# A branch over sixty no-ops at the head of VectorE's program, and a dead copy taken out, in a rotary-embedding kernel

## The chip, the core and the metric

The kernel runs on one core of a Trainium2 chip. The metric is the device time of one execution in microseconds (us); lower is better. A time is a median over several runs, and one further execution is recorded by the hardware profiler: its profile and its trace are what the text reads.

## The reference

`x` has the shape (16, 512, 1024) in float32: 16 sequences of 512 positions, each position a row of 16 heads of 64 numbers. Every head is split into its first and its second half of 32 numbers and rotated by tables of cos and sin that depend on the position alone:

```python
x = x.reshape(batch, seq, num_heads, head_dim)
x1, x2 = x[..., :half_dim], x[..., half_dim:]
cos = cos[None, :, None, :]
sin = sin[None, :, None, :]
rotated = np.concatenate([x1 * cos - x2 * sin, x1 * sin + x2 * cos], axis=-1)
```

The arithmetic is small. 33.6 MB are read and 33.6 MB are written.

## The kernel before

**Tiles.** The rows are cut into eight tiles of 4 MB. A tile holds two sequences: 128 partitions, and in each partition eight positions ("rows" `r` = 0 to 7) of 1024 numbers. A tile `x_sb` is loaded, changed in place and stored. Five buffers (`NB`) hold tiles.

**The tables.** `sin` and `cos` are loaded by ScalarE's queue into 64 partitions (`tabs`, L73 and L74). The tables have to stand in all 128 partitions, and TensorE does that: GpSimd makes an identity matrix `ident` (L80, L81), VectorE builds from it a selecting matrix `sel` and its negative (L86 to L88), and three products (L93 to L95) give `sns_ps` (−sin, +sin) and `cos_ps` (cos) in PSUM. ScalarE copies `sns_ps` to `sns` in SBUF (L99), since GpSimd works from there, and `cos_ps` to `cost` (L100). Nothing reads `cost`.

**The work on a tile** (`compute`). For every position, x times cos is added to x with its halves swapped times (−sin, +sin).
- Rows 0 and 1 (`PEROWS`): GpSimd makes the second product `B` of row 0, VectorE that of row 1 (L126). VectorE makes the first product in place (L136). TensorE adds the two by products with `ident` (L141, L142), and ScalarE copies the sums back (L143).
- Rows 2 to 7 in three pairs (`PAIRS`): GpSimd makes the second product `T` (L131), VectorE the first one into PSUM (`pp`, L147) and the sum (L148).

**Order.** The schedule is the program's order (`manual_schedule`). All transfers of x stand on SyncE's queue in one order: load 0 in four pieces, loads 1 to 4, stores 0 to 2, loads 5 to 7, stores 3 to 6, and the last store in four pieces. A load into a buffer that is used again waits for that buffer's store. At the start each engine takes part in a barrier and runs over one branch to its own part of the program (L191 in the trace); at the end SyncE waits for the last stores (also L191).

```python
    for t in range(NB):
        compute(t)
        if t < NT - NB:
            store(t)
    for t in range(NB, NT):
        load(t)
```

Of the kernel before, what the change touches and what calls it, by code (L numbers as in the profile page):

```python
# [7 lines left out]
FP32 = mybir.dt.float32  # L8
# [4 lines left out]
def kernel(  # L13
# [8 lines left out]
    nc = tc.nc  # L22
    P = nc.NUM_PARTITIONS
# [3 lines left out]
    half = hd // 2  # L27
# [4 lines left out]
    R = seq // HP  # L32
# [2 lines left out]
    NB = 5  # L35
    PAIRS = (2, 4, 6)
    PEROWS = (0, 1)

    xv = x.rearrange("b (p r) d -> (b p) (r d)", r=R)
    xv = xv.rearrange("(t p) f -> t p f", p=P)  # L40
# [5 lines left out]
    fixed = ctx.enter_context(tc.tile_pool(name="fixed", bufs=1))  # L46
# [28 lines left out]
    for t in range(1, NB):  # L75
        load(t)


    ident = fixed.tile([P, P], FP32, name="ident")
    nc.gpsimd.memset(ident, 0.0)  # L80
    nc.gpsimd.affine_select(  # L81
        out=ident, in_=ident, compare_op=ALU.not_equal, fill=1.0,
        base=0, pattern=[[-1, P]], channel_multiplier=1,
    )
    sel = fixed.tile([HP, 2, P], FP32, name="sel")
    nc.vector.tensor_copy(out=sel[:, 0, :HP], in_=ident[:HP, :HP])  # L86
    nc.vector.tensor_copy(out=sel[:, 0, HP:], in_=ident[:HP, :HP])
# [3 lines left out]
    cos_ps = ptab.tile([P, R, half], FP32, name="cos_ps")  # L91
# [3 lines left out]
    nc.tensor.matmul(out=cos_ps.rearrange("p r j -> p (r j)"), lhsT=sel[:, 0, :], rhs=tabs[:, 0],  # L95
                     start=True, stop=True)
    sns = fixed.tile([P, R, 2, half], FP32, name="sns")
    cost = fixed.tile([P, R, half], FP32, name="cost")
    nc.scalar.copy(out=sns, in_=sns_ps)  # L99
    nc.scalar.copy(out=cost, in_=cos_ps)  # L100

    def view(ap, r0, n):

        return ap[:, r0 * dim:(r0 + n) * dim]
# [5 lines left out]
    def snsb(tab, r0, n):  # L110
        return bass.AP(tensor=tab.tensor, offset=tab.offset + r0 * hd,
                       ap=[tab.ap[0], [hd, n], [0, nh], [1, hd]])

    def swapped(xt, r0, n):
        return bass.AP(tensor=xt.tensor, offset=xt.offset + r0 * dim + half,
                       ap=[xt.ap[0], [hd, n * nh], [-half, 2], [1, half]])

    def compute(t):
# [3 lines left out]

        for r in PEROWS:
            B = bpool.tile([P, dim], FP32, name="B")
            eng = nc.vector if r == PEROWS[-1] else nc.gpsimd
            eng.tensor_tensor(out=B, in0=swapped(xt, r, 1), in1=snsb(sns_ps if eng is nc.vector else sns, r, 1),  # L126
# [6 lines left out]

        for r in reversed(PEROWS):
            xr = view(xt, r, 1)
# [60 lines left out]
```

## Time and profile before

| | |
|---|---|
| median of 3 runs | 162.91 us (162.82 to 163.51) |
| profiled execution, its own time | 162.99 us |
| its span in the trace | 161.0 us |
| VectorE (DVE) busy | 137.8 us, 86% |
| GpSimd (POOL) busy | 127.1 us, 79% |
| TensorE (PE) busy | 78.3 us, 49% |
| ScalarE (ACT) busy | 21.0 us, 13% |
| HBM read and written | 33.69 MB and 33.55 MB, 418 GB/s over the span |
| SyncE's DMA queue, share of 16 DMA engines | 97.6% |

In the profile "L126" is line 126 of the kernel and "x_sb<-T,pp" an instruction that writes x_sb from T and pp. A line of a group or of the timeline names start or busy time, engine, line and operation, and in square brackets how long the engine had been idle before and who released it. A digit of the slices is the busy share of 1/40 of the span in tenths. In the DMA queues, a line is the queue's number and kind, then packets, MB and the share of the 16 DMA engines' time. "SPq" is SyncE's queue, "q14 instruction" the loading of program code. Where the text speaks of the trace's records, it means the single instructions, transfer packets and landings that the trace holds beneath these views, with their times in ns.

### The profile page before, as it was taken

What the parts mean: (1) busy time and instruction counts of PE and PEld (TensorE: products, weight loads), DVE (VectorE), ACT (ScalarE), POOL (GpSimd) and SP (SyncE); (2) the same over time, 40 slices, a digit from 0 to 9 for tenths busy, and PEclk for the clock granted to TensorE, in tenths of its full rate; (3) what the DMA queues carried; (4) which work ended last, traced back from release to release, by engine and by line L of the source; (5) the groups of instructions that cost most, each with busy time, mean ns of one, the idle gap of its engine ahead of it and who ended that gap; (6) DMA issues with size and microseconds to landing.
All of it is one profiled execution on the core that took longest, in us unless ns stands there. A gap on an engine that the chain in (4) does not pass through costs nothing. (4 is left out here: it accounts for less than half of the span.)

```text
span 161.0 us, 581 instructions
## 1 busy us (share of the span) xinstructions
PE 78.3 (49%) x134; PEld 32.3 (20%) x134; DVE 137.8 (86%) x75; ACT 21.0 (13%) x35; POOL 127.1 (79%) x38
## 2 busy tenths in 40 slices
PE   0449900598019910894049700990079803991000
PEld 0223300233014400341024200340034202340000
DVE  1077999999999999999999999999999999999400
ACT  3021210014001210022002300121001400121000
POOL 1079999999998799959995999869995999692000
PEclk9999996569755985589957995699655975598555
DMA  5999999999999999999999999999999999999994
GB/s 181 385 419 480 391 497 415 391 472 440 391 456 456 391 432 480 391 415 489 399 417 472 407 415 464 415 407 472 423 399 456 448 399 456 448 391 417 421 423 187
DMA packets 3329, 67.25 MB, mean 418 GB/s; under 512 B 384, under 2 KB 512, under 8 KB 512
## 3 DMA queue, kind: packets, MB, share of 16 engines
q1 hardware_dynamic: 3168, 67.11, 97.6%
q10 hardware_dynamic: 160, 0.13, 0.3%
q14 instruction: 1, 0.01, 0.0%
HBM read 33.69 MB, written 33.55 MB: 418 GB/s over the span
## 5 line engine op out<-in xcount | busy, mean ns | idle before, releaser
L131 POOL TENSOR_TENSOR T<-x_sb,sns 128x2048 f32<-128x2048 f32 x24 | 108.2, 4526 | 10.5 <-DVE x_sb L148 10.5
L141 PE MATMUL ps<-x_sb,ident 128*128 128x512 f32 x64 | 44.8, 790 | 61.0 <-issue 40.4
L148 DVE TENSOR_TENSOR x_sb<-T,pp 128x2048 f32<-128x2048 f32 x24 | 54.9, 2288 | 3.4 <-POOL T L131 1.0
L147 DVE TENSOR_TENSOR pp<-x_sb,cos_ps 128x2048 f32<-128x2048 f32 x24 | 55.0, 2294 | 0.6
L142 PE MATMUL ps<-B,ident 128*128 128x512 f32 x64 | 40.3, 717 | 0.0
L143 ACT COPY x_sb<-ps 128x512 f32<-128x512 f32 x32 | 18.8, 586 | 117.6 <-PE ps L142 117.6
L141 PEld LDWEIGHTS ps<-x_sb,ident 128*128 128x128 f32 x64 | 15.2, 253 | 83.3 <-issue 80.4
L126 POOL TENSOR_TENSOR B<-x_sb,sns 128x1024 f32<-128x1024 f32 x8 | 18.8, 2346 | 7.6 <-ACT sns L99 7.6
L142 PEld LDWEIGHTS ps<-B,ident 128*128 128x128 f32 x64 | 15.4, 241 | 22.0 <-issue 22.0
L136 DVE TENSOR_TENSOR x_sb<-x_sb,cos_ps 128x1024 f32<-128x1024 f32 x16 | 18.8, 1218 | 0.5
L126 DVE TENSOR_TENSOR B<-x_sb,sns_ps 128x1024 f32<-128x1024 f32 x8 | 9.7, 1217 | 7.0 <-ACT sns L99 7.0
L93 PE MATMUL sns_ps<-tabs,sel 64*128 64x256 f32 x2 | 1.2, 697 | 6.2 <-DMA tabs<-in_sin_dram 6.2
L93 PEld LDWEIGHTS sns_ps<-tabs,sel 64*128 64x128 f32 x2 | 0.5, 310 | 6.1 <-issue 6.1
L99 ACT ACT_TABLE_LOAD x1 | 1.3, 1283 | 1.9 <-issue 1.9
L86 DVE COPY sel<-ident 64x64 f32<-64x64 f32 x1 | 0.2, 185 | 1.3 <-POOL ident L81 1.3
L99 ACT COPY sns<-sns_ps 128x512 f32<-128x512 f32 x1 | 0.6, 586 | 5.0 <-PE sns_ps L94 5.0
L95 PE MATMUL cos_ps<-tabs,sel 64*128 64x256 f32 x2 | 1.2, 711 | 0.0
L94 PE MATMUL sns_ps<-tabs,sel 64*128 64x256 f32 x2 | 1.1, 631 | 0.0
L94 PEld LDWEIGHTS sns_ps<-tabs,sel 64*128 64x128 f32 x2 | 0.7, 334 | 0.2
L95 PEld LDWEIGHTS cos_ps<-tabs,sel 64*128 64x128 f32 x2 | 0.5, 306 | 0.6 <-DMA tabs<-in_cos_dram 0.6
L100 ACT COPY cost<-cos_ps 128x256 f32<-128x256 f32 x1 | 0.4, 373 | 0.5 <-PE cos_ps L95 0.5
L80 POOL MEMSET ident<- 128x128 f32 x1 | 0.2, 204 | 0.3 <-POOLq L177 0.3
(7 smaller groups left out, 1.1 us busy)
## 6 DMA issues: line engine op xcount, KB each, us to landing
x_sb<-in_x_dram SPq DMA_DIRECT2D x7, 4096.0 KB, 29.5
out_dram<-x_sb SPq DMA_DIRECT2D x7, 4096.0 KB, 27.0
x_sb<-in_x_dram SPq DMA_DIRECT2D x4, 1024.0 KB, 8.7
out_dram<-x_sb SPq DMA_DIRECT2D x4, 1024.0 KB, 9.2
tabs<-in_sin_dram ACTq DMA_DIRECT2D x1, 64.0 KB, 5.3
tabs<-in_cos_dram ACTq DMA_DIRECT2D x1, 64.0 KB, 6.7
```

The costliest lines, as they stand in the source:

```text
L93: nc.tensor.matmul(out=sns_ps[:, :, 1, :], lhsT=sel[:, 0, :], rhs=sin3, start=True, stop=True)
L94: nc.tensor.matmul(out=sns_ps[:, :, 0, :], lhsT=sel[:, 1, :], rhs=sin3, start=True, stop=True)
L95: nc.tensor.matmul(out=cos_ps.rearrange("p r j -> p (r j)"), lhsT=sel[:, 0, :], rhs=tabs[:, 0], start=True, stop=True)
L99: nc.scalar.copy(out=sns, in_=sns_ps)
L126: eng.tensor_tensor(out=B, in0=swapped(xt, r, 1), in1=snsb(sns_ps if eng is nc.vector else sns, r, 1), op=ALU.mult)
L131: nc.gpsimd.tensor_tensor(out=T, in0=swapped(xt, r0, 2), in1=snsb(sns, r0, 2), op=ALU.mult)
L136: nc.vector.tensor_tensor(out=xr, in0=xr, in1=cosb(cos_ps, r, 1), op=ALU.mult)
L141: nc.tensor.matmul(out=ps, lhsT=ident, rhs=xc, start=True, stop=False)
L142: nc.tensor.matmul(out=ps, lhsT=ident, rhs=bc, start=False, stop=True)
L143: nc.scalar.copy(out=xc, in_=ps)
L147: nc.vector.tensor_tensor(out=pp, in0=xr, in1=cosb(cos_ps, r0, 2), op=ALU.mult)
L148: nc.vector.tensor_tensor(out=xr, in0=ts[r0], in1=pp, op=ALU.add)
```

## The change

Behind the two instructions that make `ident`, VectorE gets a register set to 0 and a conditional block that is entered if the register is above 0, which it never is. In the block stand 60 no-ops. The block divides the program: each engine's instructions are now in a part before it and a part behind it. In the built program that places a plain branch on every engine: on SyncE behind the first of the four pieces of load 0, on ScalarE between the loads of sin and cos, on GpSimd between the two instructions on `ident`, on TensorE at the head. VectorE has, at its head, two register moves, the compare-and-branch, the 60 no-ops and the block's closing branch. The rest of the program keeps its order on every engine.

The copy of `cos_ps` to `cost` is gone, and the tile with it. VectorE's first product with cos (L136), which waited for ScalarE because of that copy, waits for TensorE instead.

```diff
+    PAD = 60
...
-
     ident = fixed.tile([P, P], FP32, name="ident")
     nc.gpsimd.memset(ident, 0.0)
     nc.gpsimd.affine_select(
         out=ident, in_=ident, compare_op=ALU.not_equal, fill=1.0,
         base=0, pattern=[[-1, P]], channel_multiplier=1,
     )
+
+
+    step = nc.vector.alloc_register("step")
+    nc.vector.reg_mov(step, 0)
+    with tc.If(nc.vector.snap(step) > 0):
+        for _ in range(PAD):
+            nc.vector.nop(hint="pad")
+
+
     sel = fixed.tile([HP, 2, P], FP32, name="sel")
...
     sns = fixed.tile([P, R, 2, half], FP32, name="sns")
-    cost = fixed.tile([P, R, half], FP32, name="cost")
     nc.scalar.copy(out=sns, in_=sns_ps)
-    nc.scalar.copy(out=cost, in_=cos_ps)
```

## The prediction

> **What bounds the kernel now.** I read the page first: busy shares, the slices, the DMA queues.
>
> ```profile
> PE 78.3 (49%) x134; PEld 32.3 (20%) x134; DVE 137.8 (86%) x75; ACT 21.0 (13%) x35; POOL 127.1 (79%) x38
> ...
> DMA  5999999999999999999999999999999999999994
> ...
> q1 hardware_dynamic: 3168, 67.11, 97.6%
> ...
> q14 instruction: 1, 0.01, 0.0%
> ```
>
> No compute engine is full, the 16 DMA engines are: 97.6% of the span goes to SyncE's queue, and only the first and last slice are not full. One packet of the span is not data but program code (q14). Next, the waits of SyncE's queue and the end of the chain of waits:
>
> ```profile
> SPq L64 <- DMA out_dram<-x_sb: 17.7, 2, 9.5
> ...
> SPq L191 <- DMA out_dram<-x_sb: 9.0, 4, 2.4
> ```
>
> ```profile
> 148.31 2.29 DVE x_sb L148
> ```
>
> The last compute instruction ends at 150.60 of 160.97, so the chain holds only compute and leaves 10.4 us to the transfers. At the end SyncE waits for the four pieces of the last store; by the trace's records they are through at 152.83, 155.26, 157.71 and 160.15, one each 2.44 us, the steady pace of 1 MB. The third piece is issued at 147.24 and the fourth at 150.63, so there is always something queued. Transfers set the end; VectorE, though 86% busy, does not. Then the start, by the timeline:
>
> ```profile
> 0.73 0.54 ACTq L73 DMA_DIRECT2D tabs<-in_sin_dram  x1
> ...
> 1.30 0.61 ACTq L74 DMA_DIRECT2D tabs<-in_cos_dram  x1
> 1.33 0.18 DVE L86 COPY sel<-ident 64x64 f32<-64x64 f32 x1 [1.33 <-POOL ident L81]
> ...
> 1.65 0.22 DVE L88 TENSOR_SCALAR sel<-sel 64x128 f32<-64x128 f32 x1
> ...
> 6.17 1.19 PE L93 MATMUL sns_ps<-tabs,sel 64*128 64x256 f32 x2 [6.17 <-DMA tabs<-in_sin_dram]
> ...
> 8.86 1.22 DVE L126 TENSOR_TENSOR B<-x_sb,sns_ps 128x1024 f32<-128x1024 f32 x1 [6.99 <-ACT sns L99]
> ...
> 9.30 0.37 ACT L100 COPY cost<-cos_ps 128x256 f32<-128x256 f32 x1 [0.47 <-PE cos_ps L95]
> 10.19 2.35 DVE L136 TENSOR_TENSOR x_sb<-x_sb,cos_ps 128x1024 f32<-128x1024 f32 x2
> ```
>
> VectorE has finished `sel` at 1.87 and TensorE first needs it when sin lands, at 6.13: **4.26 us of cover** for anything put at the head of VectorE.
>
> Last, where the code packet falls and how the transfers run out: the DMA queues from 81 to 83 us, and the last stretches (the last two numbers are DMA share and GB/s).
>
> ```profile
> q14 instruction: 1, 0.01, 1.0%
> ```
>
> ```profile
> 158.00:158.50 0.50, 0.00 (x0) 0.00 (x0) 0.00 (x0) 0.00 (x0) 0.00 (x0) 0.50 0.89 377
> 158.50:159.00 0.50, 0.00 (x0) 0.00 (x0) 0.00 (x0) 0.00 (x0) 0.00 (x0) 0.50 0.28 115
> 159.00:159.50 0.50, 0.00 (x0) 0.00 (x0) 0.00 (x0) 0.00 (x0) 0.00 (x0) 0.50 0.15 66
> ```
>
> The reader is to see that the engines do not stop together. By the single landings of the last piece, fourteen DMA engines are through by 159.28; one ends at 160.10 and one at 160.14. From 159.3 on the kernel waits for two of sixteen.
>
> **The change part by part.** The sum is made against the profiled execution: 162.99 us, a span of 160.97 and 2.02 around it. The median of the three runs, 162.91, is 0.08 lower, so the end result is the sum less 0.08.
>
> *The branch on VectorE.* The no-ops are jumped over. What is executed is two register moves, a compare-and-branch and its landing. The trace has no taken compare; the nearest row is the branch that already heads each engine's program: on SyncE the opening barrier's wait ends at 0.667 and the first DMA starts at 0.733, so that branch costs at most 0.07 us. Upper bound, if the target's code had to be fetched: no more than the small table loads took from issue to landing, 5.3 and 6.7 us. Either goes against 4.26 us of cover. Behind it stands more: the first piece of the last store is issued at 146.08, while the store before it keeps the engines busy until 152.83 − 2.44 = 150.39. A transfer needs 1.0 us from issue to first data (0.73 to 1.74 at the start), or 2.4 if I take the first load's 5.1 us to landing less 2.7 of moving 1 MB at 384 GB/s; that is 1.9 to 3.3 us of slack. VectorE may start 6.2 us late before anything shows, and the upper bound of 6.7 costs 0.5. I take 0.07, nearest to the program's own head branch: cost 0. If the transfers did not cover it, it would cost its whole length.
>
> *The plain branches on the other engines.* In the built program each engine gets one, to the next instruction. GpSimd's lies before the affine select (same 4.26 us), TensorE's at its head (idle to 6.13). ScalarE's lies between the sin and the cos load; cos is ready at 8.05 + 1.22 = 9.27 and VectorE asks for it at 10.19, 0.9 us of cover. SyncE's lies behind the first piece of the first load, with seven loads behind it. Second piece: issued at 1.155, data possible from 2.16; the first piece's data run from 1.74 for 2.7 us, to 4.4. Cover 2.3 us against 0.07. Cost 0.
>
> *The dead copy.* 0.37 us of ScalarE. Before, VectorE's first product with cos waited for it (to 9.67), but starts at 10.19 behind its own `B`; afterwards it waits for TensorE (9.27). Gain 0; ScalarE's next work is at 15.17.
>
> *The code packet.* VectorE's program grows by 64 instructions, and code is loaded in blocks. The packet (8192 bytes, 309 ns, at 82.13) delays its DMA engine more than its own time: the data packet after it took 1745 ns where the usual one takes 1213, 532 over, so 0.84 us in all. At the landing before it (82.08) no engine is more than 0.13 behind; at the next one two are, by 0.34 and 0.49, the fetching engine last, and at the end they are 0.82 and 0.86 behind. Whose code is it? Of the instructions in the trace VectorE had begun 63 of 119, ScalarE 32 of 62, GpSimd 38 of 62, SyncE 23 of 47. If the four load alike, only VectorE gets far enough to need a block the others never ask for (TensorE, with 152 of 291, passed 63 long before without a packet). Then the changed program reaches that border 64 instructions sooner, at about its first instruction instead of its 63rd, and the packet falls before 1.74 us, where no data run yet.
>
> The gain lies between 0 (it only moves) and 0.86 (nobody is late any more). I take 0.04: the second late engine had no code packet, lost a few ns on packet after packet from 62 us on, and would still land at 160.10. A loss is possible too: a packet more within the stream, 0.31 to 0.84 on one engine.
>
> On this the Trainium skill ("Runtime: NRT & Kernel Launch", Instruction fetch mechanics) says that running over the border of a block is mostly hidden, and names blocks of 16 KiB. By it this term would be 0; the records show 8 KiB and a delay that is never made up. The same section says that a taken branch out of the loaded blocks stalls the engine for a fetch, which speaks against the change; no row here shows such a branch.
>
> **Sum:** 162.99 − 0.04 − 0.08 = 162.87, so 162.9 us.
>
> **The rivals.**
> *Faster by the whole tail.* Without the packet in mid-stream the fetching engine is on time, and the second one's lag was this execution's chance. Then the end moves from 160.14 to 159.28: 162.05. For it: the lag starts at the packet. Against: the second engine has its own reason, which the change does not touch. Chance 0.14; about 0.12 of it beyond the bound.
> *Slower: SyncE's branch stalls on code.* It stands between the first and second load piece; with a stall s the DMA engines run dry for s − 2.3. At the 5.3 to 6.7 us of the table loads that is 3.0 to 4.4, so 165.9 to 167.3; it decides from s = 2.3 and exceeds the bound from 3.1. Against: its target is the next instruction, and the branch at the program's head cost 0.07. Chance 0.05. The extra packet in the stream (163.2 to 163.7) and a fetch at VectorE's end get 0.03 beyond the bound.
> *It does not do what it moves for.* The packet is another engine's, or comes at another time in the stream: 162.9 within 0.3. Chance 0.3, all within the bound.
> *My forecast,* the packet leaves the stream and one late engine still sets the end: 0.48.
>
> **How the numbers follow.** 0.5% of 162.91 is 0.81 us, about what a measurement of this kernel can tell from no change. Faster by more 0.12, within 0.80, slower by more 0.08. The range reaches down to the whole tail (162.05) and up by one extra packet beside the 0.6 us by which one of the three runs stood above the median: 162.0 to 163.4. That leaves out the stalled branch.
>
> **What would show it.** Right: q14 is gone from 81 to 83 us and, if it is in the span at all, stands before 2 us; the two-engine tail becomes a one-engine tail; VectorE's first product still follows the sin landing near 8.9. Wrong: a gap in the DMA slices near 4 us (SyncE's branch); VectorE's `sel` later than 6.1; a second q14 packet; fourteen engines ending later than 159.3, for then the stream's rate has changed, which no step here foresees.

## The result and the profile after

| | before | changed |
|---|---|---|
| median of 17 runs each | 162.95 us (162.80 to 163.51) | 163.70 us (163.11 to 164.67) |
| profiled execution, its own time | 162.99 | 164.30 |
| its span | 160.97 | 161.72 |
| outside the span in that execution | 2.02 | 2.58 |

The ratio is 1.0046 with a 95% interval of 1.0031 to 1.0062: slower by 0.75 us. That is within the 0.5% that the prediction called no change, but 163.70 lies above its range, and the small gain that it forecast is a loss.

The engines' work is as it was (busy times of the page of the changed kernel):

```profile
PE 77.1 (48%) x134; PEld 31.9 (20%) x134; DVE 137.8 (85%) x75; ACT 20.6 (13%) x34; POOL 127.1 (79%) x38
...
q1 hardware_dynamic: 3168, 67.11, 97.2%
...
q14 instruction: 1, 0.01, 0.0%
```

The start, by the timeline of the changed kernel. VectorE's first copy is 0.15 us later (1.33 before), TensorE still waits for sin, and VectorE's first product is even 0.06 earlier (8.86 before):

```profile
1.48 0.19 DVE L95 COPY sel<-ident 64x64 f32<-64x64 f32 x1 [1.48 <-POOL ident L81]
...
6.11 1.19 PE L102 MATMUL sns_ps<-tabs,sel 64*128 64x256 f32 x2 [6.11 <-DMA tabs<-in_sin_dram]
...
8.80 1.22 DVE L133 TENSOR_TENSOR B<-x_sb,sns_ps 128x1024 f32<-128x1024 f32 x1 [6.78 <-ACT sns L107]
```

The code packet has left 82 us. The DMA queues of the changed kernel from 5.0 to 5.5 us hold it:

```profile
q14 instruction: 1, 0.01, 3.9%
```

By the records it begins at 5.06, takes 309 ns, and the data packet behind it takes 879 where 309 is usual, 570 over. That is 0.88 us on one engine, against 0.84 at 82 us before. So it was moved, at full price, and not out of the data. The tail of the changed kernel by the stretches (last two numbers DMA share and GB/s):

```profile
158.50:159.00 0.50, 0.00 (x0) 0.00 (x0) 0.00 (x0) 0.00 (x0) 0.00 (x0) 0.50 0.36 148
159.00:159.50 0.50, 0.00 (x0) 0.00 (x0) 0.00 (x0) 0.00 (x0) 0.00 (x0) 0.50 0.08 33
159.50:160.00 0.50, 0.00 (x0) 0.00 (x0) 0.00 (x0) 0.00 (x0) 0.00 (x0) 0.50 0.08 33
160.00:160.50 0.50, 0.00 (x0) 0.00 (x0) 0.00 (x0) 0.00 (x0) 0.00 (x0) 0.50 0.04 16
```

A packet counts in the row in which it starts. The tail reaches further than before, where the row from 159.5 was empty. The last piece lands at 159.69 on the second latest engine and at 160.88 on the latest; before, both were there by 160.14. The records do not number the engines. That the latest one carried the code packet is read from its lag: it begins at the landing behind that packet and stays to the end. The span is 0.74 longer, and so is that landing (160.88 − 160.14). The other 0.57 of the profiled execution lies behind the span, where the trace still holds transfers. The DMA queues of the kernel before, from 161 to 165 us:

```profile
q8 instruction: 1, 0.02, 2.0%
q14 instruction: 1, 0.01, 0.7%
```

and of the changed kernel, from 161.7 to 165.7:

```profile
q8 instruction: 1, 0.02, 2.0%
q14 instruction: 2, 0.02, 1.3%
```

One more block of code is loaded after the end. By the records the two packets of q14 begin 1.61 and 2.37 us behind the end of the span; before, the single one began 1.05 behind it.

### The profile page after: what moved, and what is told of

Its sections match the earlier page's. It is cut to its first block, busy times and chain, and to the rows that moved or that the text cites. A ratio compares the mean times of both kernels' runs of the same rounds, so it can differ in the third digit from the quotient of the medians.

```text
span 161.7 us, 583 instructions
## 1 busy us (share of the span) xinstructions
PE 77.1 (48%) x134; PEld 31.9 (20%) x134; DVE 137.8 (85%) x75; ACT 20.6 (13%) x34; POOL 127.1 (79%) x38
## 5 line engine op out<-in xcount | busy, mean ns | idle before, releaser
L148 PE MATMUL ps<-x_sb,ident 128*128 128x512 f32 x64 | 44.1, 779 | 60.9 <-issue 42.1
L149 PE MATMUL ps<-B,ident 128*128 128x512 f32 x64 | 39.5, 705 | 0.0
L150 ACT COPY x_sb<-ps 128x512 f32<-128x512 f32 x32 | 18.8, 586 | 117.4 <-PE ps L149 117.4
## 6 DMA issues: line engine op xcount, KB each, us to landing
x_sb<-in_x_dram SPq DMA_DIRECT2D x7, 4096.0 KB, 29.9
```

The source lines that it names most:

```text
L148: nc.tensor.matmul(out=ps, lhsT=ident, rhs=xc, start=True, stop=False)
L149: nc.tensor.matmul(out=ps, lhsT=ident, rhs=bc, start=False, stop=True)
L150: nc.scalar.copy(out=xc, in_=ps)
```

## The experiments

Theory A: both parts are loading of VectorE's code. A program that is 65 instructions longer as built (188 against 123) reaches one more block at its end, and the packet inside the span moves with VectorE's instructions and makes its DMA engine late wherever it falls. Rival B: the branches themselves cost. C: the missing copy matters. D: only a code packet that falls on the start of the stream matters. E: the loss grows with the length.

Since each run gives its own time and its span, the loss can be split for every run into the span and what lies outside it (the time less the span). Before (84 runs beside the experiments): span 161.0, outside 1.95 (medians). The changed kernel: 161.2 and 2.55.

| kernel | length | code packet(s) in the span, us | latest engine behind, us | span | outside | median us, ratio |
|---|---|---|---|---|---|---|
| before | 123 | 82.1 | 1.01 | 161.0 | 1.95 | 162.95 |
| changed (60) | 188 | 5.1 | 1.76 | 161.2 | 2.55 | 163.70, 1.0046 [1.0031, 1.0062] |
| copy out only | 123 | 82.1 | 0.97 | 161.0 | 2.08 | 163.10, 0.9999 [0.9987, 1.0010] |
| 1 no-op | 129 | 82.1 | 1.13 | 161.15 | 2.03 | 163.24, 1.0016 [1.0001, 1.0030] |
| block at the end | 188 | 82.4 | 1.16 | 161.0 | 2.59 | 163.59, 1.0033 [1.0021, 1.0044] |
| no-ops executed | 183 | 7.8 | 2.15 | 162.05 | 2.05 | 164.15, 1.0065 [1.0048, 1.0082] |
| 10 | 138 | 65.2 | 0.80 | 160.75 | 2.02 | 162.78, 0.9988 [0.9975, 1.0000] |
| 20 | 148 | 55.5 | 0.95 | 160.7 | 2.04 | 162.73, 0.9977 [0.9963, 0.9991] |
| 20 again | 148 | 55.6 | 0.93 | 160.75 | 2.05 | 162.81, 0.9983 [0.9970, 0.9996] |
| 28 | 156 | 42.0 | 2.68 | 162.3 | 2.03 | 164.30, 1.0071 [1.0048, 1.0094] |
| 40 | 168 | 29.9 | 1.41 | 162.05 | 2.09 | 164.20, 1.0072 [1.0045, 1.0100] |
| 55 | 183 | 5.0 | 1.89 | 161.7 | 2.04 | 163.82, 1.0037 [1.0015, 1.0059] |
| 72 | 200 | 5.0 and 154.5 | 2.21 | 162.2 | 2.04 | 164.23, 1.0068 [1.0045, 1.0090] |
| 100 | 228 | 4.9 and 117.4 | 1.86 | 161.7 | 2.01 | 163.71, 1.0053 [1.0022, 1.0084] |

The length is the number of instructions of VectorE's built program. "Behind" is, in the profiled execution, the last of the sixteen landings of the last piece less the eighth. A single traced execution need not be the median one: that with 40 no-ops had a span of 161.5. Ratios are to the kernel before on the same chip.

**The dead copy alone**, taken out of the kernel before.

```diff
-    cost = fixed.tile([P, R, half], FP32, name="cost")
-    nc.scalar.copy(out=cost, in_=cos_ps)
```

> Only the dead copy of cos is taken out; VectorE's program keeps its length and nothing branches. Theory A (the change's loss is code loading: VectorE's program is 65 instructions longer and runs over one more block of code, mostly after the span): 162.95 us, within 0.15 of the kernel before, 2.0 us outside the span, one code packet near 82 us. Rival B (the branches themselves cost): also 162.95. Rival C (the missing copy lets VectorE or ScalarE run differently and that costs): 163.4 or more.

Measured 163.10, ratio 0.9999, packet at 82.09. The copy was worth nothing, and C falls.

**The branches without the length.** This and the kernels below are edits of the changed one.

```diff
-    PAD = 60
+    PAD = 1
```

> The changed kernel with one no-op in the block in place of 60: all branches, register moves and the compare are there, but VectorE's program is only 6 instructions longer than before. Theory A: no loss, 162.95 within 0.2; outside the span 2.0 us as before; the code packet comes a few instructions earlier, near 70 to 82 us. Rival B (the branches cost, on VectorE or where they split the loads on SyncE and ScalarE): 163.5 to 163.7 as in the changed kernel.

Measured 163.24: outside the span 2.03, packet at 82.07. All the branches, register moves and the compare are there, and at most 0.3% of loss is left, with an interval that begins at nothing. B does not carry the loss. The packet was expected a few instructions earlier and did not move.

**The length at the end of VectorE's program.** The block from `alloc_register` to the no-ops is moved behind the last `store`.

```diff
     for t in range(NB, NT):
         compute(t)
         store(t, pieces=4 if t == NT - 1 else 1)
+
+    step = nc.vector.alloc_register("step")
+    nc.vector.reg_mov(step, 0)
+    with tc.If(nc.vector.snap(step) > 0):
+        for _ in range(PAD):
+            nc.vector.nop(hint="pad")
```

> The dead copy is out, and the same branch over 60 no-ops stands at the end of VectorE's program, behind its last sum, in place of its head. Theory A: outside the span 2.3 to 2.6 us as in the changed kernel (before 2.0), the span as before with its code packet near 82 us: 163.3 to 163.6. Rival B (the branches at the head cost): 162.95. Rival D (the loss is a code packet that falls on the start of the stream): 162.95 too, since the packet is back at 82 us.

Measured 163.59, with the span of before (161.0) and 2.59 outside. Behind its span (161.1 to 165.1 us) the DMA queues show the second packet again, as in the changed kernel and in no other:

```profile
q14 instruction: 2, 0.02, 1.6%
```

This parts the two terms: the end of the program costs about 0.6 us with no branch and no no-ops at its head (0.5 against the other edited kernels, which lie at 2.01 to 2.09 outside). D, which expected 162.95 here, falls.

**The length without a branch.**

```diff
-    step = nc.vector.alloc_register("step")
-    nc.vector.reg_mov(step, 0)
-    with tc.If(nc.vector.snap(step) > 0):
-        for _ in range(PAD):
-            nc.vector.nop(hint="pad")
+    for _ in range(PAD):
+        nc.vector.nop(hint="pad")
```

> The dead copy is out, and the 60 no-ops stand at the head of VectorE's program with no branch around them, so they are executed: length without branches. VectorE's sel comes later by 60 times the issue of a no-op, 2 to 3 us by the 20 to 50 ns of its register moves and waits, within the 4.26 us of cover. Theory A: as the changed kernel, 163.4 to 163.8, of it 2.3 to 2.6 us outside the span, and a code packet in the first 6 us. Rival B: 162.95.

The loss is larger than expected (164.15), and not where I put it: outside the span 2.05, inside it 1.05 us more, and the packet at 7.8 us and not in the first 6. The built length is 183, five short of the changed kernel's, and the end then reaches no further block. The timeline of this kernel shows that the head itself is covered: `sel` ends at 4.48 instead of 1.87, and VectorE's first product starts within 0.04 us of before.

```profile
4.26 0.22 DVE L94 TENSOR_SCALAR sel<-sel 64x128 f32<-64x128 f32 x1
...
8.90 1.22 DVE L130 TENSOR_TENSOR B<-x_sb,sns_ps 128x1024 f32<-128x1024 f32 x1 [4.43 <-ACT sns L104]
```

So a kernel with the packet at 7.8 us has 1.05 us more of span with no branch anywhere, and one at 82 us is what the kernel before already pays. That asked for the packet to be moved in steps.

**The packet in steps.** Only the number changes:

```diff
-    PAD = 60
+    PAD = 20    # and 40, 72, 100, then 55, 10, 28, and 20 once more
```

> The changed kernel with 20 no-ops: VectorE's program is 148 long as built (before 123, changed kernel 188, 60 executed no-ops 183). Theory A, now in two terms: what lies outside the span is +0.5 only where the program's end reaches a further block (188 did, 183 did not), so 2.0 us here; inside the span the one code packet comes about 25 instructions earlier than before, from VectorE's place near 35, 43 to 50 us, and is served one or two packets behind the end of a transfer, so near 43 or 53 us. The earlier it falls the longer its engine is late: span 161.0 to 161.6, 163.1 to 163.6 us. Rival B (each branch costs by itself): as with one no-op, 163.2, with a span of 161.1 wherever the packet falls. Rival E (the loss grows with the length): 163.2.

> 40 no-ops, 168 long. Theory A: 2.0 us outside the span; packet from VectorE's place near 15, 13 to 20 us, served behind the end of a transfer, near 13.5 or 23 us; span 161.2 to 162.1, 163.2 to 164.1 us. Rival B: 163.2. Rival E (the loss grows with the length): 163.4 to 163.5, with part of the 0.5 us outside the span.

> 72 no-ops, 200 long: longer than the changed kernel. Theory A: the first block border now lies ahead of the span, and the next one, 128 instructions on, falls inside the program near VectorE's place 105 to 112, 130 to 145 us; the end reaches no further block: 2.0 us outside the span, code packet at 140 to 151 us, span 160.8 to 161.3, 162.8 to 163.3 us, less than the changed kernel though the program is longer. Rival E (the loss grows with the length): 163.8 or more, 2.5 us outside the span.

> 100 no-ops, 228 long. Theory A: as with 72, the packet from VectorE's place 77 to 84, 98 to 108 us, so near 101 or 111 us; 2.0 us outside the span, span 160.8 to 161.3, 162.8 to 163.3 us. Rival E (the loss grows with the length): 164 or more.

With 20 no-ops the kernel is faster than both, 162.73 us, a case that no theory had named. With 40 it loses 1.05 us of span, as with the executed no-ops. With 72 and 100 the outside is back at 2.04 and 2.01 as expected, so E falls: the longest programs do not pay the end's 0.6 us, only 188 does, and 228 loses less than 200, 168 and 156. Their times, though, were expected at 163.3 or less and came out at 164.23 and 163.71. I had put the first packet ahead of the span; it stayed at 5 us, and a second one came at 154.5 and 117.4, here in the queues of the kernel with 72 from 154 to 155 us:

```profile
q14 instruction: 1, 0.01, 1.9%
```

Two packets, two delays: in the traced execution with 72 the latest engine is 1.45 us behind at 151.8 and 2.21 at the end.

The packet's place follows VectorE's instructions through the row 1, 10, 20, 28, 40, 55: 82.1, 65.2, 55.5, 42.0, 29.9, 5.0 us. It is VectorE's code. A count shows it more sharply. Take VectorE's instructions that the trace shows begun when the packet comes, and add the no-ops jumped over. The first packet comes at 63 to 67 in every kernel whose packet lies at 7.8 us or later, and the second one, with 72 and 100, at 191 and 194. The jumps over 55 and more no-ops land close to the first place or behind it, and all four such kernels have their packet near 5 us. By the same count the programs with a length of 188 end at 182, a little short of the second place, and the two with 183 at 177 and 179; with 72 and 100 that place is passed inside the span. That is in line with an extra block behind the end of the first alone, though the count by itself does not say why 182 is near enough to ask for it and 179 is not.

That the packet is served just behind the end of a transfer, as I expected from 82 us, does not hold: the others fall in the middle of one.

The traces then suggested why an early packet costs more. SyncE's stream turns from loads to stores twice, after load 4 (near 51 us) and after load 7 (near 110). At these turns the late engine's last load packets are stretched. The lag of the latest engine is taken here for each transfer, its last landing less its eighth. With the changed kernel this lag is 0.72 us up to the first turn, 0.95 after it, 1.00 before the second and 1.77 after it, where one of its packets took 2128 ns instead of 1213. The next four kernels were made to test that.

> 55 no-ops, 183 long as built: the length at which 60 executed no-ops cost nothing outside the span, with the branch of the changed kernel. Theory A: 2.0 us outside the span (changed kernel 2.5), the code packet still early, between 5 and 14 us, before the stream turns from loads to stores near 50 us; span 161.2 to 162.2, 163.2 to 164.2 us, scattered. Rival E (the loss grows with the length): 2.4 us outside.

> 10 no-ops, 138 long. Theory A: 2.0 us outside the span; the code packet behind the end of a transfer near 62 or 72 us, after the first turn from loads to stores (50 us): span 160.6 to 161.1, 162.6 to 163.1 us, as with 20. If 20 no-ops were faster by chance: 163.0 to 163.2.

> 28 no-ops, 156 long. The packet should move ahead of the turn from loads to stores near 50 us, to 33 or 43 us. Theory A (an engine made late before that turn is stretched there once more): span 161.4 to 162.1, 163.4 to 164.1 us, as with 40. Against it (what counts is only the packet itself, 0.85 us): span 160.7 to 161.1, 162.7 to 163.1 us.

> The kernel with 20 no-ops once more, since it was 0.23% faster than the kernel before. If that was no chance: 162.6 to 162.9 us, span 160.5 to 160.9, packet at 53 to 56 us. If it was chance: 163.0.

55 and 10 came out in time and span as theory A had it (the packet with 10 was expected near 62 or 72 us and came at 65.2), 20 repeated its gain, and 28 lost even more than expected (162.3 us of span, expected at most 162.1). The sharpest comparison is 28 against 20: eight no-ops more move the packet from 55.5 to 42.0 us, across the first turn, and cost 1.5 us. The two packets, one from 42 to 43 us with 28 and one from 55 to 56 with 20:

```profile
q14 instruction: 1, 0.01, 2.0%
```

```profile
q14 instruction: 1, 0.01, 2.0%
```

In the trace with 28 the late engine is 0.93 us behind after the packet, 1.62 after the first turn (its packet at 51.50 took 2133 ns) and 2.62 after the second (2255 ns at 109.30). With 20 the lag is 0.77 after the packet and 0.85 after the second turn; with 10, 0.73 and 0.69. The growth is uneven, though: with 40 no-ops the first turn adds 0.04 only (0.94 to 0.98) and the second 0.35 (0.99 to 1.34), and with 100 the first adds 0.02 (0.70 to 0.72). The tail with 28 no-ops, by the stretches:

```profile
160.00:160.50 0.50, 0.00 (x0) 0.00 (x0) 0.00 (x0) 0.00 (x0) 0.00 (x0) 0.50 0.08 33
160.50:161.00 0.50, 0.00 (x0) 0.00 (x0) 0.00 (x0) 0.00 (x0) 0.00 (x0) 0.50 0.08 33
```

and in the second run with 20:

```profile
159.00:159.50 0.50, 0.00 (x0) 0.00 (x0) 0.00 (x0) 0.00 (x0) 0.00 (x0) 0.50 0.04 16
159.50:160.00 0.50, 0.00 (x0) 0.00 (x0) 0.00 (x0) 0.00 (x0) 0.00 (x0) 0.50 0.00 0
```

In the one, data packets still start behind 160.5; in the other the last one ends at 159.57, with the same bytes and the same compute.

With 55 the changed kernel's early packet is there and the end's extra block is not: outside 2.04, span 161.7, scattered from 160.4 to 162.5. The 20 no-ops, run twice, are the version that beats both kernels, by 0.17 and 0.23% against the kernel before.

## Why the prediction was wrong

**The bound held.** The last landing comes 0.83 to 0.84 us before the end of the span in every traced execution here, so transfers set the end. VectorE's head had the cover that the text gave it: 2.6 us of delay there with the executed no-ops moved its first product by 0.04.

**The branches and the copy held.** SyncE's second load piece is issued at 1.169 (1.155 before), so the rival that would stall there is refuted. The copy alone gives a ratio of 0.9999. Of the signs that were named, q14 left 81 to 83 us and the two-engine tail became one engine's, as forecast; that the packet would stand before 2 us did not come true, and a second q14 packet came, behind the span.

**The step that failed is the code packet.** Its owner was right (VectorE) and its price was right (0.84 us before, 0.88 after). Wrong was the sentence that it falls "before 1.74 us, where no data run yet". VectorE was at its first instructions by 1.80 and then stood in a wait until 5.73, but the packet was served at 5.06, when data had long been moving: at least 3.2 us later, and 4.15 behind the compare (0.905). So it stayed in the stream, ahead of two turns instead of one, and the term was not −0.04 but +0.2 us at the median and +0.74 in the profiled execution. I had the engine's lag only as something that the packet sets once; in the changed kernel it more than doubles from the packet to the end (0.72 to 1.76), and it grows at the two turns from loads to stores.

The size of the term, 0.04, rested on a second late engine that would still land at 160.10. That did not hold either: the second latest landing is at 159.69 in the changed kernel and at 159.44 to 159.90 in the traced executions of the others.

**The second term had been named and then priced at next to nothing.** "A fetch at VectorE's end" shared a chance of 0.03 with another mishap. It is the larger part: 0.6 us outside the span (2.55 against 1.95). The prediction counted which code border VectorE passes inside the span and did not carry the same count on to the end of the longer program. That the extra block causes the 0.6 us is read from its place: the two kernels that have it are the two that pay. Together the medians give 162.95 + 0.2 + 0.6 = 163.75, against 163.70 measured.

**The rule that was weighed.** The Trainium skill ("Runtime: NRT & Kernel Launch", Instruction fetch mechanics) calls running over a block's border mostly hidden. For VectorE that agrees: its last instruction ends at 150.53 us in the changed kernel and at 150.60 before. What pays is the DMA engine that carries the block (0.88 us), in a kernel whose end is set by the latest of sixteen.

**What stays open.** Why a late engine's packet is stretched at a turn was not tried by itself: that the others already store while it still loads fits the place, and is argued only. A rival is that the packet with 28 falls among loads and those with 10 and 20 among stores. The kernel before speaks against it: its packet, at 82.1 us, stands at the head of loads 5 to 7, and its span of 161.0 is much nearer to theirs (160.7) than to that with 28 (162.3). No run was made for it alone. What the packet waited for until 5.06 us is open too: in the four kernels that jump over 55 or more no-ops it comes 4.0 to 4.15 us behind the compare, so it may have stood behind queued data or may take about that long in any case. Early packets cost 0.2 us of median span in the changed kernel and 0.7 with 55 no-ops, both with packets near 5 us; spans scatter by 1.3 and 2.1 us there, so that difference is not explained. Nor is it settled why 10 and 20 no-ops are better than the kernel before, whose packet also falls between the turns: in the profiled executions the eighth landing of the last piece comes at 158.9 to 159.1 us in all of them, and the latest engine is 0.80 to 0.95 behind instead of 1.01. With only the copy out, and the packet at 82.1 us too, it is 0.97 behind, so these single executions do not show where the gain lies.

## What to carry to other kernels

Where the DMA engines are full from end to end, the end is that of the latest one: look at the sixteen landings of a transfer, not only at the mean share, and ask what made one engine late and when. Code is a transfer too: a change in the number of an engine's instructions, executed or not, moves the place where the next block is loaded, in the stream and behind the end, so a change of length is to be followed to the last instruction. A time that moves by a few tenths of a per cent with an edit that does nothing may be such a packet; shift it with a few no-ops before believing in the edit.

## What the runs showed of the hardware that was not expected

- One code packet of 8192 bytes takes 309 to 333 ns, but the data packet behind it on its DMA engine takes 0.35 to 0.66 us more than usual.
- Where the jump at the head passes the border, the code packet comes microseconds behind it (compare at 0.905 us, packet at 5.06; 4.0 to 4.15 us in four kernels).
- At a turn from loads to stores, packets of 32 KB took up to 2.26 us instead of 1.21, and where a code packet lay ahead of the turn, the lag of the latest engine grew there by 0.01 to 0.97 us.
- The extra block behind the end was loaded at a built length of 188 and not at 183, nor at 200 or 228: a longer program need not pay it.
- VectorE's first instruction behind the compare starts at 1.34 us with 20, 40 or 55 no-ops in the block and at 1.48 with 60, 72 or 100 (the compare is at 0.905 to 0.908 in all of them).
